# A two-block transformer in fp32 on one core: output turned tile by tile at the end, modulation in three pieces, strict order where the norm's steps run

## The chip, the cores and the metric

The kernel runs on one core of a Trainium2 chip. The metric is device time in microseconds, median of three runs. The engines are TensorE (PE, matmuls; PEld its weight loads), VectorE (DVE), ScalarE (ACT), GpSimd (POOL) and SyncE (SP), which issues the DMAs. A 128-partition memory (SBUF) feeds the engines, and matmuls write to PSUM.

## The reference

256 latent tokens (`x`) and 256 context tokens, width 1024, go through two blocks of two layers each. The first block's layers look like this (its second layer gives no context output):

```python
mod = silu_c @ w_mod[l] + b_mod[l]                     # 6 x 1024 per stream
sh1, sc1, g1, sh2, sc2, g2 = jnp.split(mod, 6)
a = modulate(rms_norm(h, norm1_g[l]), sh1, sc1)        # y * (1 + scale) + shift
p, u, vs, q, k, v, gl = jnp.split(a @ w_in[l], SPLIT_POINTS)
# three branches: pooling mix, spatial gating, neighbourhood attention over latent + context
h = h + g1 * merge_branches(...)
h = h + g2 * sq_relu_mlp(modulate(rms_norm(h, norm2_g[l]), sh2, sc2), w_ff1[l], w_ff2[l])
# at the block's end: rms_norm(h, final_g)
```

The second block has one layer with an mLSTM mixer (two directions, chunks of 128) and one with sliding-window attention (SWA, 16 heads, window 128, sinks), each with modulation and MLP (width 4096) in the same manner, and ends with `rms_norm(h, final_g)` of the 256 latent tokens, which is the output (256 x 1024).

## The kernel before

**Layout.** The residual lies transposed in SBUF as `h[128, 8, 512]`: eight row tiles `k` of 128 features, columns 0 to 255 the context, 256 to 511 the latent tokens. A matmul in fp32 is made of three: each operand is split into a high part (`whi`, by an ACT copy, L118) and a low part (`wlo`, by a subtraction, `split`, L132); high x high, high x low and low x high are added up in PSUM. A weight tile is 128 x 1024 (512 KB), loaded by SP (`staged`, L143), and its halves are made by ACT and, as `wlow` says, by DVE or POOL.

**Order.** The kernel is written in Python in the order wanted; a list scheduler puts each engine's instructions in order: among those that are ready in its own model of the machine, the earliest written goes first (`sooner` moves some up). An engine then works its queue strictly in that order. `issue_after(ins)` adds an edge to the scheduler's order alone: what is written under it is queued behind `ins`.

**Gemms.** `gemm` (L209) runs over weight tiles; `rows_of` (L164) writes, for each of the eight rows of an accumulation, the three matmuls (`mm`, L124). A group's first tiles may run side by side (`head`), the second two rows behind the first (SKEW). The last tiles of a gemm (`last_tiles`, L246) run the latent columns of all tiles first and then the context columns, so that the latent tokens' norm may start early. `Steps` (L47) is that norm as a Python generator, whose steps are taken at given ticks (rows) of other matmuls: `MID` (6, 12) in the second stream of the last tiles, `PRE` (4, 7) in the first matmuls of the next group ("head"), where the context's norm runs. Only where an instruction is given as `after` are the rows chained in written order.

**Norm.** `square` makes the squares by row tile (ACT, then sums on POOL, L551; the last two tiles by a pair addition on DVE, L558). `variance` (L564) makes the mean square per token in a column of PSUM, a power on POOL (L569), `rows` spreads it by four matmuls over partitions, and `modulate` makes the next group's inputs.

**Modulation.** For each of the four layers a vector of 1024 is multiplied with 1024 x 6144 weights, 352 units of 128 x 512 that are popped from a list (`pending`). A unit (L464) is a load of 256 KB, a product-addition on DVE into `a0` (context), a product on ACT and an addition on POOL into `a1` (latent, L480); after eight units 16 small matmuls and a reading out follow. `drip` (L502) pops units at a `rate` per weight tile; `need` pops what is missing before a value is used. There are three buffers for the loads and one pair of accumulators.

**Places.** `block1` (L873) is called twice (l = 0, 1); its context norm in layer 1 runs whole after the first three weight tiles. `block2_swa` (L1354) sets `wlow` to POOL for the weights of the query tiles. At the end of `build` the factor of the final norm is spread by `rows` over all partitions, eight DVE operations scale the row tiles and eight DMAs write the output transposed (`out_T`, L1471); the host turns it.

Of the kernel before, what the change touches and what calls it, by code (L numbers as in the profile page):

```python
# [19 lines left out]
P = 128  # L20
D = 1024
KT = 8
# [15 lines left out]
FIRST = (3, 3, 3, 3, 5, 7, 7, 7, 7), (2, 2, 2, 2, 4, 6, 6, 6, 6), (1, 1, 1, 1, 3)  # L38

WARM = 40  # L40
PRE, MID = (4, 7), (6, 12)
PLAIN = (3, 6)

SOONER = 70
# [2 lines left out]
class Steps:  # L47
# [5 lines left out]
    def tick(self):  # L53
# [3 lines left out]
            ins = next(self.parts, None)  # L57
        return ins

    def finish(self):  # L60
        for _ in self.parts:
            pass


class Builder:
    def __init__(self, tc, io, stack):
        self.tc, self.nc, self.io = tc, tc.nc, io
        self.n = 0
        self.pending, self.owed, self.rate = [], 0.0, 0.0
        self.raws = cycle(["raw"])  # L70
# [93 lines left out]
    def rows_of(self, pss, tiles, ks_of, xs, r0, r1, a, e, steps=None, after=None):  # L164

        last = len(xs) - 1
        order = after and (lambda ins=after: self.tc.issue_after(ins.ins))
        strict = bool(after)  # L170
        for i in range(r0, r1 + SKEW * (len(tiles) - 1)):
            for j, (ps, (d, w)) in enumerate(zip(pss, tiles)):
                i0 = i - SKEW * j
                if not r0 <= i0 < r1:
                    continue
                k = ks_of(d)[i0]
                wh, wl = (x[:, k * P:(k + 1) * P] for x in w)
                xh, xl = (x[:, a:e] for x in xs[i0])
                with order() if order else nullcontext():
                    self.mm(ps, wh, xh, start=(i0 == 0), stop=False)  # L180
                    self.mm(ps, wh, xl, start=False, stop=False)
                    ins = self.mm(ps, wl, xh, start=False, stop=(i0 == last))
            if strict:
                with self.tc.issue_after(ins.ins):
                    part = steps.tick()
                ins = part or ins
                order = lambda ins=ins: self.tc.issue_after(ins.ins)
            elif steps:
                steps.tick()
        return ins  # L190

    def group(self, tiles, ks_of, xs, cols, evac, steps=None):


        for a, e in cols:
            pss = [self.ps(next(self.banks))[:, :e - a] for _ in tiles]
            self.rows_of(pss, tiles, ks_of, xs, 0, len(xs), a, e, steps)
            self.flush()
            self.take(pss, tiles, a, e, evac)

    def take(self, pss, tiles, a, e, evac):

# [4 lines left out]
                    self.late.append(part)  # L207

    def gemm(self, aps, xs, c0, evac, head=0, tail=0, order=(LAT, CTX), pre=None, mid=None, flush=True,  # L209
             ahead=(), streams=True):  # L210

# [7 lines left out]
        while i < n - tail:  # L219
            m = max(head, 1) if i == 0 else 1  # L220
            cols = by_stream if streams and m > 1 and not self.ready else [(c0, T)]
            tiles = [(i + j, self.ready.pop(0) if self.ready else self.wload(aps[i + j], kt))
                     for j in range(m)]
            if i + m == n:
                self.ready = [self.wload(ap, KT) for ap in ahead]
            steps = Steps(pre, PRE) if pre and i == 0 else None
            self.group(tiles, ks_of, xs, cols[:1], evac, steps)
            if steps:
                steps.finish()
            self.group(tiles, ks_of, xs, cols[1:], evac)  # L230
            for _ in range(1 if m == 1 else 0 if streams else m):
                self.drip()
            i += m
# [11 lines left out]

    def last_tiles(self, tiles, ks_of, xs, by_stream, evac, mid):  # L246
        steps = Steps(mid, MID) if mid else None
        for s, cols in enumerate(by_stream):
            for tile in tiles:
                self.group([tile], ks_of, xs, [cols], evac, steps if s else None)  # L250
        if steps:
            steps.finish()

# [204 lines left out]
    def mod_units(self, i, groups):  # L458
# [3 lines left out]
        w, sc = self.io[f"wmod{i}"], self.silu[i // 2]  # L462

        def unit(cg, half, k):  # L464
            raw = self.staged(w[cg, k][:, half * 512:half * 512 + 512], 512, cycle(["mraw"]))
            a0, a1 = self.macc[:, 0], self.macc[:, 1]

            alone = i % 2 == 1 and cg >= 2
            if not alone or k % 2 == 0:
                s = LAT if alone else CTX  # L470
                if k == 0:
                    self.nc.vector.tensor_scalar_mul(a0, raw, sc[:, k, s:s + 1])
                else:
                    self.stt(a0, raw, sc[:, k, s:s + 1], a0, ALU.mult, ALU.add)
            if not alone or k % 2:
                if k < 2 - (not alone):
                    self.act(a1, raw, scale=sc[:, k, LAT:LAT + 1])
# [17 lines left out]
        out = []  # L495
        for cg in groups:
            for half in range(2):
                out += [((i, cg), (lambda cg=cg, half=half, k=k: unit(cg, half, k)))
                        for k in range(KT)]
        return out  # L500

    def drip(self):  # L502
# [5 lines left out]
        self.owed = min(self.owed, 1.0)  # L508

    def one(self):  # L510
        self.pending.pop(0)[1]()

    def need(self, i, cg):

        while any(key == (i, cg) for key, _ in self.pending):
            self.one()
        while self.late:
            self.flush()

# [181 lines left out]
        return evac  # L701


    def mlp(self, i, xs, c0, tag, pre=None, mid=None, other=None, gain=None, rows=None):


        w1, w2 = self.io[f"ff1_{i}"], self.io[f"ff2_{i}"]
# [37 lines left out]
            hid[q] = hs  # L745

        def down(q, **kw):
            self.gemm2([w2[q, d] for d in range(4)], hid.pop(q), c0, self.add_to_h(g2, q == 7, gain), **kw)

        self.raws = cycle(["raw", "Y", "Y"])  # L750
        up(0, head=3, pre=pre)
# [121 lines left out]
def block1(b, ph, l, xs, pre, after):  # L873
# [12 lines left out]
        b.perm1 = b.load(ph, "perm1")  # L886
        b.icnt = b.load(ph, "icnt")
    pscale = b.vec[l][:, 64:66]
    b.rate = 0.0 if l else RATES[l][0]
    win = io[f"win{l}"]  # L890

    qs, kh, kl = [], [], []
# [55 lines left out]
    if l == 0:  # L948
        pre(evac_first)
    else:  # L950
        b.gemm(aps[:3], xs, c0, evac_first, head=3)
        b.ready = [b.wload(ap, KT) for ap in aps[3:]]
        b.whole(pre)
        b.gemm(aps[3:4], xs, c0, lambda j, *r: evac_first(j + 3, *r))
    b.gemm_rows(aps[4:], L, xs, ("T", "T", "S", "S")[c0 // P:], evac_vs, c0=c0)
    br = b.new_xs("B", 4)
# [394 lines left out]
    b.mlp(i, xs, 0, "A", pre=b.norm(xs, CTX, A, S), **after)  # L1351


def block2_swa(b, ph, xs, pre):  # L1354
    nc, io = b.nc, b.io
    i = 3
    rope2 = b.load(ph, "rope2")
# [35 lines left out]
    def project(t):  # L1393
        b.gemm([win[t]], xs, L, lambda _, ps, a, e: qs.append(query(ps)))

    b.wlow = nc.gpsimd
    project(0)
    for t in range(8):
        if t < 7:
            project(t + 1)  # L1400
        a = b.new_xs("A", 1)[0]
# [19 lines left out]
    b.mlp(i, xs, L, "A", pre=b.factors(R), rows=R)  # L1421


def build(tc, io):
    from contextlib import ExitStack

    with ExitStack() as stack:
# [35 lines left out]
            st, pre, mid = follow(3, "B")  # L1463
            block2_mlstm(b, ph, xs2, b.norm_twice(xs2, A, S), dict(mid=mid))
        with tc.tile_pool(name="b3", bufs=1) as ph:
            block2_swa(b, ph, st["xs"], pre())
        R = b.rstd_rows(LAT)
        for k in range(KT):
            t = b.T1()
            b.stt(t, b.h[:, k, L:], b.fin[:, 8 + k:9 + k], R, ALU.mult, ALU.mult)  # L1470
            nc.sync.dma_start(io["out"][:, k, :], t)  # L1471

# [149 lines left out]
```

## Time and profile before

| | |
|---|---|
| runs | 2252.66, 2251.72, 2252.01 us; median 2252.01 |
| profiled execution | 2251.2 us, span 2249.3 us, 36790 instructions |
| mean granted clock of TensorE | 0.986 |
| PE busy | 2179.0 us, 97% |
| DVE busy | 1617.5 us, 72% |
| ACT busy | 1155.4 us, 51% |
| POOL busy | 642.3 us, 29% |

The span is the time from the profile's first to its last instruction on the core. Busy times are the sums of an engine's own instructions; PE's matmuls are pipelined, and their ends are modelled. The granted clock is the share of TensorE's full speed that it was given: 1.00 in most of the span, lower in a few stretches. In a timeline's row stand the start in us, the busy time in us, engine, line, operation, output<-inputs by the program's names, shape and count; a bracket gives the engine's idle time before it and what ended that.

### The profile page before, as it was taken

How to read it: one execution, taken by the hardware profiler on the slowest of the kernel's cores; microseconds unless marked ns; L12 is line 12 of the kernel's file. 1: busy time of each engine (PE TensorE's matmuls, PEld its weight loads, DVE VectorE, ACT ScalarE, POOL GpSimd, SP SyncE). 2: the span in 40 equal slices, each digit the busy share in tenths (PEclk: the TensorE clock that was granted, in tenths of full speed). 3: DMA queues.
4: the chain of work that ended last, by engine and by line, in shares of the span. 5: the costliest groups of instructions: out<-in, count | busy, mean ns of one | idle time of the engine just before them, and what ended most of it. 6: DMA issues, size and time to landing. Idle time of an engine off the chain costs nothing.

```text
span 2249.3 us, 36790 instructions
## 1 busy us (share of the span) xinstructions
PE 2179.0 (97%) x13602; PEld 1861.3 (83%) x13602; DVE 1617.5 (72%) x2830; ACT 1155.4 (51%) x2176; POOL 642.3 (29%) x529
## 2 busy tenths in 40 slices
PE   9899999999999989998999999999999999999998
PEld 7777877887777778898999977778777778879998
DVE  5876656777666986789777766678775566697776
ACT  4556434544443456655555665645444433676453
POOL 1630534524221542045000234262232122421000
PEclk9999999999999999999999999999999999999999
DMA  8451535445565443367554323444455552214552
GB/s 296 140 167 36 169 122 190 144 133 183 191 193 162 147 154 127 120 215 254 166 186 151 113 85 104 142 142 131 137 187 177 173 168 80 76 48 143 186 179 93
DMA packets 129011, 337.86 MB, mean 150 GB/s; under 512 B 15040, under 2 KB 24256, under 8 KB 128832
## 3 DMA queue, kind: packets, MB, share of 16 engines
q1 hardware_dynamic: 128832, 335.51, 46.0%
q8 instruction: 108, 1.77, 0.3%
q14 instruction: 71, 0.58, 0.1%
HBM read 334.40 MB, written 1.05 MB: 149 GB/s over the span
## 4 chain that ended last, share of the span: by engine, by line
PE 46%; DVE 4%; ACT 2%; issue 2%; POOL 1%; DMA 0%; DVEq 0%; POOLq 0%; ACTq 0%
PE mm L124 28%; PE mx L124 11%; PE S L124 2%; PE T L124 1%; PE num L124 1%; PE pv L124 1%; PE T L128 1%; DVE wlo L132 1%; ACT whi L118 1%; PE acc L124 0%; POOL macc L480 0%; DMA mraw<-wmod_in 0%; PE kv L124 0%; DVE B L121 0%; ACT W L118 0%
## 5 line engine op out<-in xcount | busy, mean ns | idle before, releaser
L124 PE MATMUL mm<-A,whi 128*128 128x512 f32 (+2 forms) x2632 | 666.2, 340 | 4.9 <-DVE A L121 1.5
L480 POOL TENSOR_TENSOR macc<-macc,mraw 128x512 f32<-128x512 f32 x244 | 361.9, 1483 | 757.3 <-ACT mraw L118 744.8
L124 PEld LDWEIGHTS mm<-A,whi 128*128 128x128 f32 x2632 | 449.3, 190 | 69.0 <-issue 10.0
L124 PE MATMUL mm<-B,whi 128*128 128x512 f32 (+2 forms) x1916 | 461.4, 331 | 2.8 <-DVE h L121 1.0
L132 DVE TENSOR_TENSOR wlo<-raw,whi 128x1024 fp32r<-128x1024 f32 x255 | 350.8, 1378 | 140.7 <-ACT whi L118 139.6
L124 PE MATMUL mm<-A,wlo 128*128 128x512 f32 (+2 forms) x1316 | 444.4, 338 | 1.2 <-DVE wlo L132 1.2
L118 ACT ACTIVATE whi<-raw 128x1024 fp32r<-128x1024 f32 x267 | 281.2, 1055 | 250.5 <-PE mm L124 154.6
L124 PEld LDWEIGHTS mm<-B,whi 128*128 128x128 f32 x1916 | 322.1, 189 | 41.8 <-issue 3.0
L118 ACT ACTIVATE mraw<-mraw,silu 128x512 f32<-128x512 f32 x244 | 175.5, 723 | 303.1 <-DVE macc L121 181.3
L124 PE MATMUL mx<-A,whi 128*128 128x512 f32 (+2 forms) x1272 | 323.3, 341 | 5.5 <-ACT whi L118 4.2
L124 PE MATMUL mm<-B,wlo 128*128 128x512 f32 (+2 forms) x958 | 315.2, 330 | 1.1 <-DVE wlo L132 1.1
L121 DVE SCALAR_TENSOR_TENSOR macc<-mraw,silu,macc 128x512 f32<-128x512 f32 x244 | 250.2, 1025 | 58.8 <-DMA mraw<-wmod_in 56.3
L124 PEld LDWEIGHTS mm<-A,wlo 128*128 128x128 f32 x1316 | 249.4, 190 | 29.2 <-DVE wlo L132 2.0
L132 DVE TENSOR_TENSOR wlo<-Y,whi 128x1024 fp32r<-128x1024 f32 x160 | 207.7, 1298 | 78.7 <-ACT whi L118 78.5
L118 ACT ACTIVATE whi<-Y 128x1024 fp32r<-128x1024 f32 x160 | 168.9, 1055 | 177.8 <-PE mm L124 124.7
L124 PEld LDWEIGHTS mx<-A,whi 128*128 128x128 f32 x1272 | 218.6, 190 | 35.1 <-ACT whi L118 4.4
L124 PE MATMUL mx<-A,wlo 128*128 128x512 f32 (+2 forms) x636 | 216.3, 340 | 0.7 <-DVE wlo L132 0.7
L124 PE MATMUL mx<-B,whi 128*128 128x256 f32 (+2 forms) x852 | 203.9, 327 | 3.0 <-DVE B L121 1.3
L124 PEld LDWEIGHTS mm<-B,wlo 128*128 128x128 f32 x958 | 181.1, 189 | 19.9 <-DVE wlo L132 2.0
L121 DVE SCALAR_TENSOR_TENSOR h<-mm,mod,h 128x256 f32<-128x256 f32 x278 | 125.5, 478 | 65.0 <-PE mm L124 64.6
L124 PEld LDWEIGHTS mx<-B,whi 128*128 128x128 f32 x852 | 144.3, 191 | 19.9 <-DVE B L121 2.7
L551 POOL TENSOR_TENSOR sums<-sums,T 128x256 f32<-128x256 f32 x60 | 65.6, 1100 | 307.5 <-ACT T L118 306.3
(331 smaller groups left out, 3009.8 us busy)
## 6 DMA issues: line engine op xcount, KB each, us to landing
mraw<-wmod_in SPq DMA_DIRECT2D x352, 256.0 KB, 2.9
Y<-ff_in SPq DMA_DIRECT2D x160, 512.0 KB, 3.6
raw<-ff_in SPq DMA_DIRECT2D x96, 512.0 KB, 3.5
raw<-win_in SPq DMA_DIRECT2D x68, 512.0 KB, 3.8
raw<-mwin_in SPq DMA_DIRECT2D x17, 512.0 KB, 3.5
raw<-wo_in SPq DMA_DIRECT2D x16, 512.0 KB, 4.3
raw<-swin_in SPq DMA_DIRECT2D x10, 512.0 KB, 3.5
B<-wfirst_in SPq DMA_DIRECT2D x16, 256.0 KB, 6.7
```

The source lines that it names most:

```text
L118: return self.nc.scalar.activation(out, in_, func, **kw)
L121: return self.nc.vector.scalar_tensor_tensor(out, a, scalar, b, op0, op1)
L124: return self.nc.tensor.matmul(out, lhsT=lhsT, rhs=rhs, start=start, stop=stop, **kw)
L128: return self.nc.tensor.transpose(out, in_, self.ident[:k, :k])
L132: (eng or self.nc.vector).tensor_sub(lo, src, hi.bitcast(F32))
L480: self.nc.gpsimd.tensor_add(a1, a1, raw)
L551: (adder or self.nc.gpsimd).tensor_add(sums, sums, sq)
```

## The change

Six things are done:

1. In the last MLP each finished row tile of the residual is scaled by the final norm's gain (ACT) and transposed by two matmuls into four PSUM banks, written behind the next tile's matmuls. At the end the variance is kept per partition (token), four 128 x 512 copies out of PSUM scale by it (two on DVE, two on ACT), and four DMAs of 256 KB write the output, which has its final layout.
2. A modulation unit is a generator of three pieces: the load, the DVE product, the rest (ACT, POOL). Popping a unit writes the rest of the unit before, the loads of this one and the next one, and this one's DVE product.
3. Wherever steps run, the rows are chained as written and the steps are queued behind their tick; in the last tiles' second stream the chain goes from tile to tile until the steps are done, and MID is (8, 14).
4. In layer 1 of the first block the context's norm runs as steps at ticks 2 and 5 of the first three tiles' matmuls, and the next weights are loaded ahead.
5. The modulation's rate is 0 at the beginning of both of the first block's layers, before only of the second.
6. In SWA, `wlow` is POOL from the query tile t = 2 on; the low halves of the first two query tiles' weights are made on DVE.

```diff
-PRE, MID = (4, 7), (6, 12)
+PRE, MID = (4, 7), (8, 14)
+NEXT = (2, 5)
...
+    def done(self):
+        return self.n >= self.at[-1]
...
-        strict = bool(after)
+        strict = bool(after or steps)
...
                 order = lambda ins=ins: self.tc.issue_after(ins.ins)
-            elif steps:
-                steps.tick()
         return ins
...
-            self.rows_of(pss, tiles, ks_of, xs, 0, len(xs), a, e, steps)
+            ins = self.rows_of(pss, tiles, ks_of, xs, 0, len(xs), a, e, steps, after)
...
-            steps = Steps(pre, PRE) if pre and i == 0 else None
+            steps = Steps(pre, at) if pre and i == 0 else None
...
+        last = None
         for s, cols in enumerate(by_stream):
             for tile in tiles:
-                self.group([tile], ks_of, xs, [cols], evac, steps if s else None)
+                due = s and steps and not steps.done()
+                ins = self.group([tile], ks_of, xs, [cols], evac, steps if due else None,
+                                 last if due else None)
+                last = ins
...
         def unit(cg, half, k):
             raw = self.staged(w[cg, k][:, half * 512:half * 512 + 512], 512, cycle(["mraw"]))
+            yield
             a0, a1 = self.macc[:, 0], self.macc[:, 1]
...
                     self.stt(a0, raw, sc[:, k, s:s + 1], a0, ALU.mult, ALU.add)
+            yield
             if not alone or k % 2:
...
     def one(self):
-        self.pending.pop(0)[1]()
+        self.rest()
+        self.begun = self.pending.pop(0)[1]
+        for piece in [self.begun] + [u for _, u in self.pending[:1]]:
+            if piece not in self.loaded:
+                next(piece)
+                self.loaded.append(piece)
+        self.loaded.remove(self.begun)
+        next(self.begun)
+
+    def rest(self):
+        if self.begun:
+            next(self.begun, None)
+        self.begun = None
 
     def need(self, i, cg):
         while any(key == (i, cg) for key, _ in self.pending):
             self.one()
+        self.rest()
...
-    b.rate = 0.0 if l else RATES[l][0]
+    b.rate = 0.0
...
-        b.gemm(aps[:3], xs, c0, evac_first, head=3)
-        b.ready = [b.wload(ap, KT) for ap in aps[3:]]
-        b.whole(pre)
+        b.gemm(aps[:3], xs, c0, evac_first, head=3, pre=pre, at=NEXT, ahead=aps[3:])
...
-    b.wlow = nc.gpsimd
     project(0)
     for t in range(8):
+        if t == 1:
+            b.wlow = nc.gpsimd
...
-        R = b.rstd_rows(LAT)
-        for k in range(KT):
-            t = b.T1()
-            b.stt(t, b.h[:, k, L:], b.fin[:, 8 + k:9 + k], R, ALU.mult, ALU.mult)
-            nc.sync.dma_start(io["out"][:, k, :], t)
+            outs = []
+            def turned(k):
+                if not outs:
+                    outs.extend(b.ps(tag) for tag in ("S", "S", "acc", "T"))
+                t = b.T1()
+                b.act(t, b.h[:, k, L:], scale=b.fin[:, 8 + k:9 + k])
+                def rest():
+                    cols = slice(k % 4 * P, (k % 4 + 1) * P)
+                    for j in range(2):
+                        b.tr(outs[2 * (k // 4) + j][:, cols], t[:, j * P:(j + 1) * P])
+                b.late.append(rest)
+            block2_swa(b, ph, st["xs"], pre(), turned)
+            b.flush()
+            r = b.variance(LAT)
+            for half in range(2):
+                for j in range(2):
+                    o, ps, f = b.t("W" if half else "E"), outs[2 * half + j], r[:, j:j + 1]
+                    if j:
+                        b.act(o, ps, scale=f)
+                    else:
+                        nc.vector.tensor_scalar_mul(o, ps, f)
+                    nc.sync.dma_start(
+                        io["out"][j * P:(j + 1) * P, half * T:(half + 1) * T], o)
```

## Rows read from the trace of the kernel before

**Rows 1.** The page, parts 1 and 5: busy times; POOL's modulation additions.

```profile
PE 2179.0 (97%) x13602; PEld 1861.3 (83%) x13602; DVE 1617.5 (72%) x2830; ACT 1155.4 (51%) x2176; POOL 642.3 (29%) x529
...
L480 POOL TENSOR_TENSOR macc<-macc,mraw 128x512 f32<-128x512 f32 x244 | 361.9, 1483 | 757.3 <-ACT mraw L118 744.8
```

**Rows 2.** Windows: length, PE, PEld, DVE, ACT, POOL busy, clock, DMA share, GB/s.

```profile
50.00:100.00 50.00, 44.27 (x263) 37.29 (x262) 41.83 (x54) 25.03 (x42) 30.79 (x23) 0.93 0.43 136
800.00:850.00 50.00, 41.89 (x293) 37.83 (x292) 43.82 (x73) 27.40 (x48) 20.68 (x21) 0.90 0.45 151
1500.00:1550.00 50.00, 44.71 (x329) 42.16 (x328) 39.67 (x69) 25.73 (x52) 18.91 (x15) 0.93 0.35 109
1700.00:1750.00 50.00, 50.00 (x229) 39.72 (x228) 29.41 (x44) 20.80 (x30) 11.17 (x8) 1.00 0.56 177
1900.00:1950.00 50.00, 43.96 (x288) 41.30 (x287) 28.26 (x58) 25.53 (x57) 19.17 (x14) 0.86 0.26 85
```

**Rows 3.** Timeline of the end, from the last matmul on.

```profile
2237.97 0.28 PE L124 MATMUL mx<-A,wlo 128*128 128x256 f32 x1
...
2240.84 0.71 POOL L569 TENSOR_TENSOR sm<-sm,m 128x2 f32<-128x2 f32 x1 [3.58 <-DVE sm L568]
...
2242.35 3.22 DVE L121 SCALAR_TENSOR_TENSOR T<-h,fin,T 128x256 f32<-128x256 f32 x8 [1.59 <-PE T L124]
2242.86 3.79 SPq L1471 DMA_DIRECT2D out_T<-T  x8
```

**Rows 4.** Instructions of line 128 (transposes): ns min/median/max, first and last start.

```profile
L128 PE MATMUL T<-ident,T x48: 270/270/421, 21.4 to 1878.3; 128*128 128x128 f32 x48
```

**Rows 5.** Timeline in SWA: four transposes in a row.

```profile
1960.62 0.60 PE L128 MATMUL T<-ident,E 128*128 128x128 f32 x4
```

**Rows 6.** Timeline at layer 0's beginning.

```profile
81.29 0.72 ACT L118 ACTIVATE mraw<-mraw,silu 128x512 f32<-128x512 f32 x1 [4.28 <-DVE sm L942]
82.86 0.57 ACT L118 ACTIVATE E<-mm 128x512 f32<-128x512 f32 x1
83.49 1.22 PE L124 MATMUL T<-E,perm 128*128 128x256 f32 x2 [5.73 <-ACT E L118]
...
90.13 0.68 DVE L966 TENSOR_TENSOR B<-S,sgb 128x512 f32<-128x512 f32 x1
```

**Rows 7.** DMA issues: count, KB each, median us to landing.

```profile
mraw<-wmod_in SPq DMA_DIRECT2D x352, 256.0 KB, 2.9
...
B<-wfirst_in SPq DMA_DIRECT2D x16, 256.0 KB, 6.7
...
out_T<-T SPq DMA_DIRECT2D x8, 128.0 KB, 2.0
```

**Rows 8.** Timeline of PE at layer 1's start.

```profile
831.16 1.22 PE L124 MATMUL mx<-A,whi 128*128 128x512 f32 x2 [4.19 <-ACT whi L118]
...
835.24 0.58 PE L124 MATMUL S<-wlo,A 128*128 128x256 f32 x1 [2.85 <-DVE wlo L132]
```

**Rows 9.** Timeline in the mLSTM layer's tail.

```profile
1508.82 0.75 DVE L121 SCALAR_TENSOR_TENSOR macc<-mraw,silu,macc 128x512 f32<-128x512 f32 x1 [3.19 <-DMA mraw<-wmod_in]
...
1512.12 0.53 PE L124 MATMUL T<-mean,T 128*128 128x1 f32 x2 [3.69 <-DVE T L558]
```

**Rows 10.** Timeline at SWA's first query tiles.

```profile
1919.76 2.37 POOL L132 TENSOR_TENSOR wlo<-raw,whi 128x1024 fp32r<-128x1024 f32 x1 [4.22 <-ACT whi L118]
...
1923.76 0.39 PE L124 MATMUL mm<-whi,B 128*128 128x256 f32 x1 [2.06 <-ACT T L118]
...
1940.98 0.49 PE L124 MATMUL S<-Q,Q 128*128 128x512 f32 x1 [1.64 <-DVE Q L121]
```

**Rows 11.** Timeline of DVE in the first MLP's head.

```profile
437.70 1.21 DVE L132 TENSOR_TENSOR wlo<-Y,whi 128x1024 fp32r<-128x1024 f32 x1
```

**Rows 12.** The chain of waits: start, us, a run of 48 matmuls of 128x256.

```profile
1929.70 5.70 PE mm L124 x48
```

**Rows 13.** Window of the first MLP's head, columns as in rows 2.

```profile
434.00:447.00 13.00, 12.15 (x105) 11.07 (x103) 11.83 (x24) 8.28 (x19) 3.76 (x3) 1.00 0.37 121
```

More of the change, by code (lines that the diff above doesn't have):

```diff
@@ L69, in __init__ @@
         self.pending, self.owed, self.rate = [], 0.0, 0.0
+        self.begun, self.loaded = None, []
         self.raws = cycle(["raw"])
@@ L187, in rows_of, with group @@
                 order = lambda ins=ins: self.tc.issue_after(ins.ins)
-            elif steps:
-                steps.tick()
-        return ins
-    def group(self, tiles, ks_of, xs, cols, evac, steps=None):
+        return ins
+    def group(self, tiles, ks_of, xs, cols, evac, steps=None, after=None):
+        ins = None
         for a, e in cols:
             pss = [self.ps(next(self.banks))[:, :e - a] for _ in tiles]
-            self.rows_of(pss, tiles, ks_of, xs, 0, len(xs), a, e, steps)
+            ins = self.rows_of(pss, tiles, ks_of, xs, 0, len(xs), a, e, steps, after)
             self.flush()
             self.take(pss, tiles, a, e, evac)
+        return ins
     def take(self, pss, tiles, a, e, evac):
@@ L209, in gemm @@
     def gemm(self, aps, xs, c0, evac, head=0, tail=0, order=(LAT, CTX), pre=None, mid=None, flush=True,
-             ahead=(), streams=True):
+             ahead=(), streams=True, at=PRE):
         kt, n = len(xs), len(aps)
@@ L497, in mod_units @@
             for half in range(2):
-                out += [((i, cg), (lambda cg=cg, half=half, k=k: unit(cg, half, k)))
-                        for k in range(KT)]
+                out += [((i, cg), unit(cg, half, k)) for k in range(KT)]
         return out
@@ L701, in add_to_h, with mlp @@
         return evac
-    def mlp(self, i, xs, c0, tag, pre=None, mid=None, other=None, gain=None, rows=None):
+    def mlp(self, i, xs, c0, tag, pre=None, mid=None, other=None, gain=None, rows=None, then=None):
         w1, w2 = self.io[f"ff1_{i}"], self.io[f"ff2_{i}"]
@@ L747, in down @@
         def down(q, **kw):
-            self.gemm2([w2[q, d] for d in range(4)], hid.pop(q), c0, self.add_to_h(g2, q == 7, gain), **kw)
+            self.gemm2([w2[q, d] for d in range(4)], hid.pop(q), c0, self.add_to_h(g2, q == 7, gain, then if q == 7 else None), **kw)
         self.raws = cycle(["raw", "Y", "Y"])
@@ L1351, in block2_mlstm, with block2_swa @@
     b.mlp(i, xs, 0, "A", pre=b.norm(xs, CTX, A, S), **after)
-def block2_swa(b, ph, xs, pre):
+def block2_swa(b, ph, xs, pre, then):
     nc, io = b.nc, b.io
@@ L1420, in block2_swa @@
     R = []
-    b.mlp(i, xs, L, "A", pre=b.factors(R), rows=R)
+    b.mlp(i, xs, L, "A", pre=b.factors(R), rows=R, then=then)
 def build(tc, io):
@@ L1465, in build @@
         with tc.tile_pool(name="b3", bufs=1) as ph:
-            block2_swa(b, ph, st["xs"], pre())
-        R = b.rstd_rows(LAT)
-        for k in range(KT):
-            t = b.T1()
-            b.stt(t, b.h[:, k, L:], b.fin[:, 8 + k:9 + k], R, ALU.mult, ALU.mult)
-            nc.sync.dma_start(io["out"][:, k, :], t)
+            outs = []
[21 more added lines that the diff above has]
+                        io["out"][j * P:(j + 1) * P, half * T:(half + 1) * T], o)
 def _tiles(w):
@@ L1617 @@
                             kind="ExternalInput").ap() for n, v in arrays.items()}
-    io["out"] = nc.dram_tensor("out_T", (P, KT, L), F32, kind="ExternalOutput").ap()
+    io["out"] = nc.dram_tensor("out_T", (L, D), F32, kind="ExternalOutput").ap()
     with tile.TileContext(nc) as tc:
@@ L1622 @@
     out = np.asarray(r.results[0]["out_T"])
-    return np.ascontiguousarray(out.transpose(2, 1, 0).reshape(1, L, D))
+    return np.ascontiguousarray(out.reshape(1, L, D))
```

## The prediction

> **What bounds the kernel now.** The page's busy times come first: TensorE (PE) is busy 97% of the span, the vector engine 72%, and the modulation's POOL additions (244 of 1483 ns) are a long side stream [rows 1]. A change that leaves the matrix work as it is can only gain in the remaining 3%, or in the clock. So the stretches of 50 us come second: in 1700 to 1750 PE is busy for all 50 us at a clock of 1.00, while around the block boundaries it is busy for 41.9 to 44.7 us of 50 and the granted clock averages 0.86 to 0.93 [rows 2]. At such places PE waits some microseconds, and then works for a while at the lower of its two levels, 1.2 instead of 2.4 GHz. What the low level costs I read as (1 - granted) times the window: 3.5 us in 50 to 100, 5.0 in 800 to 850, 3.5 in 1500 to 1550, 7.0 in 1900 to 1950. Third, the timelines of these places give the waits themselves; each part below has its own. Last, after the final matmul a tail of 11 us runs with PE nearly empty [rows 3].
>
> The sums go against the profiled execution: 2251.2 us, of which 2249.3 span and 1.9 around it. The median of the runs shown is 2252.0, 0.8 above; I add that at the end.
>
> **The end.** Before: the last matmul ends at 2238.25, its residual tile, square and variance follow; the power on POOL ends at 2241.55; four matmuls spread the factor over the partitions, eight DVE products of 0.40 us make the tiles, eight DMAs go out, the last issued at 2246.65; the span ends at 2249.3, so 2.65 us after that issue [rows 3]. The change removes the spreading and the eight products. In their place stand two rounds of scaled 128x512 copies out of PSUM, one on DVE beside one on ACT. Such a copy took 0.57 us on ACT and such an operation 0.68 on DVE [rows 6], so 2241.55 + 2 x 0.7 = 2243.0 and the last issue at about 2243.1, 3.5 earlier. The DMAs are 256 KB instead of 128 KB: before, 2.0 us to landing for the 128 KB; 256 KB took 2.9 as a median of the modulation's loads and 6.7 in the crowd at the start [rows 7]. That is 0.9 to 4.7 more. Added on the path: 16 transposes, 14 of them among the last matmuls, the last two after the last residual tile, beside the squares. One lone transpose lasts 0.27 us [rows 4], but four in a row 0.60 [rows 5], a step of (0.60 - 0.27)/3 = 0.11 us; 14 x 0.11 = 1.5. The eight ACT copies that feed them lie beside the matmuls of the following tile. Gain 3.5 - 0.9 - 1.5 = 1.1; with the slow landing -2.7, with transposes wholly under the wait for the weights +2.6. I take **+1**, nearest to the loads with the same long rows.
>
> [...]
>
> **Rate 0 at layer 0's beginning.** Nine of the modulation's units (a load, a DVE product, an ACT product, a POOL addition) no longer run before the v projection's matmuls; all later ones are up to ten units later. At 83.5 PE waits 5.73 us for ACT's E, which stood on ACT behind a unit's product that itself had waited 4.28 us for DVE [rows 6]. The low clock then costs 3.5 us [rows 2]. Ends: nothing, if E's other producers are as late, and 5.7 + 3.5 = 9.2. The units are only one of the two things on that chain, so I take **+4**.
>
> **Layer 1's start.** The context's norm no longer runs whole between the third and the fourth weight tile, but in the first three tiles' matmuls. PE's waits there are 4.19 us and 2.85 us [rows 8], and the low clock costs 5.0. The ends are +12 and, if the same DVE work merely delays the three tiles' own weight halves, +1. I take **+7**: the vector engine is busy 43.8 of 50 us [rows 2], so the work is not free, but the matmuls of three tiles cover it.
>
> **mLSTM's tail.** Of the units, what ran into this tail is now either done earlier (the output projection's gate must be complete before it, which forces a burst of some eight units there) or later. The wait is 3.69 us at 1512.1, behind a DVE pair addition that came after a unit's DVE product, which had waited 3.19 us for its load [rows 9]. With the load issued one unit ahead and the product apart from the rest, that wait should go: +3.7, and some of the 3.5 us of clock. Against it stands the burst of eight POOL additions of 1.48 = 12 us beside the matmuls of the gates. From 0 to +7; **+4**.
>
> **SWA's first two query tiles.** Their weights' low halves move from POOL to DVE. A POOL half took 2.37 us [rows 10], one on DVE 1.21 [rows 11]. PE's waits there are 2.06 and 1.64 us [rows 10], and the low level costs another 3 to 4 of the stretch's 7. DVE gets two more instructions of 1.21 in a stretch in which it is busy 28 of 50 us. 0 to +7; **+4**.
>
> **Strict order in tails and heads.** In the tails the norm's steps come 2 ticks later; a tick is three 128x256 matmuls at 0.119 us [rows 12], so 0.7 us later. In the next group's head PE may no longer take rows in any order: the matmuls are queued behind the steps in their order. Four heads of this kind (at about 434, 815, 1523, 1902). In the first the rows of the new tiles start about where the window of [rows 13] does, and PE then runs the first tile's rows ahead, since the next tile's low half is made only at 437.70 + 1.21 = 438.9 [rows 11]; in the 13 us from 434 PE is busy 12.15, idle 0.85 [rows 13]. As written, three rows of the first tile are nine matmuls, 1.07 us, until 435.1; then it waits up to 3.8 us for the second tile. Only if DVE makes the half earlier is the wait shorter, and DVE is busy 11.83 of those 13 us [rows 13]. What speaks for less: the steps' own matmuls no longer go ahead of rows that could run, and the modulated tiles come in the order in which the rows want them. Per head 0 to -4; I take -2, between, and four times that: **-8**.
>
> **The rest**, the units in three pieces elsewhere: their products stand on DVE, ACT and POOL all the same, PE is saturated beside them (clock 1.00, [rows 2]): **0**, within 3 either way.
>
> Sum: 1 + 4 + 7 + 4 + 4 - 8 = 12. 2251.2 - 12 = 2239.2, plus 0.8: **2240 us**. Taken alone this case has 2229 to 2250, some two thirds of each term up or down.
>
> **Rivals.**
> A, slower: the strict heads starve PE. Each waits 3.8 us, and PE then falls to 1.2 GHz for a stretch that costs 3.5 (as in 50 to 100 and 1500 to 1550, after waits of 5.7 and 3.7). Four times 7.3 is 29; the gains of 20 leave -9: 2261. It decides by when the second tile's low half is there: from some 3 us after the first tile's nine matmuls on. For it: DVE's fullness in these heads. Against: the low half can be put ahead of the modulated tiles on DVE, as it has slack afterwards.
> B, no change: the waits only move. E, the gate's load and the first query halves have a second producer nearly as late; early rate and mLSTM give 0, SWA 2, layer 1 4, the end 1, against -6: +1, 2251. For it: at 83.5 ACT's product before E was itself waiting for DVE [rows 6], and this DVE work partly stays.
> C: every wait and its half clock goes (2.6 + 9 + 12 + 7 + 7, of which I leave four fifths, 30) and the heads cost nothing: 2222. For it: the waits' listed releasers are just what the change moves. Against: so far as DVE is the bottleneck in 800 to 850, moving its work does not shrink it.
>
> **How the numbers follow.** Forecast 0.50, A 0.19, B 0.18, C 0.13. The range reaches from C's place to just beyond A's: 2222 to 2262. This kernel's measurement tells 0.2%, 4.5 us, from no change: same is 2247.5 to 2256.5. Of the forecast's 0.50 some 0.06 lies there; of B nearly all, 0.02 of it on either side taken together; of A 0.01. Faster 0.44 + 0.13 + 0.01 = 0.58, same 0.06 + 0.16 + 0.01 = 0.23, slower 0.19.
>
> **What would show it.** The 50 us windows at 50, 800, 1500 and 1900 should have a higher granted clock than 0.93, 0.90, 0.93, 0.86 and PE busier; 83.5's wait under 3 us; the waits of 4.19 and 2.85 at layer 1's start gone or under 2 together; 1512's under 1; the tail from last matmul to end under 11 us, transposes included. Wrong it is if PE's idle before the second tile's first row in the heads at 434, 815, 1523 and 1902 adds up to over 10 us, or if the clock falls in the head at 434, where it was 1.00 [rows 13].

## The result, and the profile after

The changed kernel takes 2268.8 us (median of four runs, 2264.5 to 2271.0) beside 2251.9 for the kernel before: a ratio of 1.0076, interval 1.0061 to 1.0091. It is slower by 17 us where 12 less were forecast. The profiled execution has a span of 2267.2, 17.9 more than before, and takes 2268.97.

The page's busy times of the changed kernel: PE is busy 8.5 us longer than in [rows 1], and in a span longer by 17.9 it is idle 9.4 us more. The granted clock of the whole span is 0.983 instead of 0.986; (1 - granted) times the span, that is some 7 us more. So about half of the loss is new waiting, and most of the other half is work done at the lower clock.

```profile
PE 2187.5 (96%) x13614; PEld 1870.0 (82%) x13614; DVE 1610.8 (71%) x2826; ACT 1162.1 (51%) x2186; POOL 623.7 (28%) x527
```

Its windows (columns as in [rows 2]) show where:

```profile
50.00:100.00 50.00, 43.51 (x248) 37.10 (x247) 43.55 (x53) 24.98 (x42) 30.76 (x23) 0.93 0.41 130
400.00:450.00 50.00, 43.84 (x303) 40.13 (x302) 34.38 (x55) 24.24 (x45) 28.43 (x23) 0.90 0.47 151
800.00:850.00 50.00, 42.55 (x311) 40.91 (x310) 40.43 (x70) 26.52 (x52) 22.64 (x22) 0.86 0.49 156
1500.00:1550.00 50.00, 45.33 (x314) 41.73 (x314) 35.30 (x59) 24.28 (x47) 27.60 (x22) 0.93 0.44 140
1900.00:1950.00 50.00, 45.31 (x336) 43.58 (x336) 29.78 (x64) 25.11 (x57) 9.77 (x11) 0.90 0.17 57
```

Against [rows 2] the places that were to get better stay where they were: the clock is 0.93 again at 50, 0.86 instead of 0.90 at 800, 0.93 again at 1500, and a little better only at 1900. And a new one has come: the stretch 400 to 450, which in the kernel before has PE busy 48.59 us at a clock of 1.00:

```profile
400.00:450.00 50.00, 48.59 (x360) 44.03 (x359) 41.05 (x68) 26.65 (x52) 27.12 (x21) 1.00 0.45 143
```

Where the time is lost is best seen as a lag: at equal sums of matmul columns done by PE, how much later than the kernel before a kernel is (worked out from all PE records of the two traces; single traces differ by up to some 4 us without cause, see the last section).

```
us before    changed   units alone   rate alone   strict alone   without strict
   402        -0.8        +2.0          -1.6          -2.1            -1.2
   463        +6.8        +6.6          +2.4          -0.1            +2.5
   793        +8.0        +5.8          +3.4          -0.7            +3.2
   892       +13.5        +5.7          +4.6          +1.1            +4.5
  1021       +12.2        +8.2          +5.1          +1.3            +3.7
  1086       +17.3       +11.2         +15.9          +1.9            +9.5
  1288       +17.1       +11.2         +16.3          +2.4            +9.1
  1324       +13.0       +16.4         +12.2          -0.5            +5.1
  1607       +15.7       +16.3         +13.7          +0.2            +6.0
  2211       +18.2       +16.3         +15.6          +2.4            +4.7
```

The first loss is 7.6 us between 402 and 463. Its timeline in the changed kernel, DVE and then PE:

```profile
421.35 1.48 DVE L127 SCALAR_TENSOR_TENSOR macc<-mraw,silu,macc 128x512 f32<-128x512 f32 x1 [1.45 <-DMA mraw<-wmod_in]
422.99 0.75 DVE L127 SCALAR_TENSOR_TENSOR macc<-mraw,silu,macc 128x512 f32<-128x512 f32 x1 [0.17 <-DMA mraw<-wmod_in]
424.95 0.75 DVE L127 SCALAR_TENSOR_TENSOR macc<-mraw,silu,macc 128x512 f32<-128x512 f32 x1 [1.22 <-DMA mraw<-wmod_in]
425.62 0.48 DVE L127 SCALAR_TENSOR_TENSOR h<-mm,g,h 128x256 f32<-128x256 f32 x1
426.92 1.53 DVE L585 TENSOR_TENSOR T<-T,T 128x256 f32<-128x256 f32 x1 [0.82 <-POOL macc L493]
...
428.51 0.59 PE L130 MATMUL T<-mean,T 128*128 128x1 f32 x2 [3.33 <-DVE T L585]
...
442.64 0.39 PE L130 MATMUL mx<-A,wlo 128*128 128x256 f32 x1 [2.72 <-DVE wlo L138]
...
821.71 0.38 PE L130 MATMUL T<-mean,sums 128*128 128x1 f32 x2 [2.40 <-POOL sums L578]
...
1539.05 0.39 PE L130 MATMUL mm<-B,wlo 128*128 128x256 f32 x1 [2.91 <-DVE wlo L138]
...
1920.11 0.58 PE L130 MATMUL mm<-B,wlo 128*128 128x256 f32 x1 [2.29 <-DVE wlo L138]
```

Two things are to be seen. At 421 to 425 the modulation's products stand on DVE ahead of the residual tile `h` and wait for their loads; so the last residual tile, the pair addition behind it and PE's variance come late, 3.33 us. It is just the wait of [rows 9], in another layer. The other four are the four heads: PE waits 2.7, 2.4, 2.9 and 2.3 us, 10.3 together, in three of them for the second tile's low half, as rival A has it, and at 821.71 for POOL's sums.

### The profile page after: what moved, and what is told of

Read it like the earlier page. It is cut to its first block, busy times and chain, and to the rows that moved or that the text cites. A ratio compares the mean times of both kernels' runs of the same rounds, so it can differ in the third digit from the quotient of the medians.

```text
span 2267.2 us, 36808 instructions
## 1 busy us (share of the span) xinstructions
PE 2187.5 (96%) x13614; PEld 1870.0 (82%) x13614; DVE 1610.8 (71%) x2826; ACT 1162.1 (51%) x2186; POOL 623.7 (28%) x527
## 5 line engine op out<-in xcount | busy, mean ns | idle before, releaser
L493 POOL TENSOR_TENSOR macc<-macc,mraw 128x512 f32<-128x512 f32 x244 | 353.8, 1450 | 663.4 <-ACT mraw L124 652.5
```

Of the source, the lines that this page charges most:

```text
L493: self.nc.gpsimd.tensor_add(a1, a1, raw)
```

## The experiments

Each ratio is to runs of the kernel before on the same chip. "Alone" is the kernel before with one part of the change.

| run | what | ratio, interval |
|---|---|---|
| end_alone | the end | 1.0008 (0.9998, 1.0017) |
| units_alone | units in three pieces | 1.0090 (1.0075, 1.0105) |
| strict_alone | strict order, MID | 1.0037 (1.0015, 1.0059) |
| without_strict | change less strict order and MID | 1.0038 (1.0024, 1.0052) |
| units_ahead | only the load a pop ahead | 0.9986 (0.9975, 0.9998) |
| units_late | only the rest a pop late | 1.0081 (1.0063, 1.0099) |
| next_alone | layer 1's start | 0.9997 (0.9984, 1.0010) |
| without_units | change less units | 1.0098 (1.0083, 1.0113) |
| rate_alone | rate 0 | 1.0077 (1.0057, 1.0096) |
| without_rate | change less rate 0 | 1.0113 (1.0092, 1.0135) |
| without_units_rate | change less both | 1.0024 (1.0012, 1.0036) |
| ahead_end_next | ahead, end, layer 1's start | 1.0000 (0.9986, 1.0013) |
| rate_made_up | rate 0, then 1.65 for 1.4 | 1.0033 (1.0020, 1.0045) |
| rate_lower | 1.2 for 1.4 in layer 0's attention | 1.0050 (1.0030, 1.0070) |
| strict_pool | strict order, low halves on POOL | 1.0059 (1.0037, 1.0081) |
| swa_alone | SWA's low halves | 0.9989 (0.9979, 0.9999) |
| ahead_swa | ahead, SWA | 0.9988 (0.9974, 1.0001) |
| ahead_swa_end | ahead, SWA, end | 0.9978 (0.9966, 0.9989) |

**First: which part?** After the traces I held that the strict order costs the time (theory S), with the units' pieces as the rival (theory U). Four kernels: the end alone, the units alone, the strict order alone (the hunks of the change's diff for that part), and the changed kernel with `strict = bool(after)`, the tails unchained and MID (6, 12).

> Only the end of the kernel as changed (row tiles turned one by one, factor per partition), all else as before. In the changed kernel the tail from the last residual matmul on is 2.7 us shorter than its lag before it would make it. Both theories: 2 to 3 us faster than before, 2249 to 2250, and no other place of the trace moves.

> Only the modulation's units in three pieces, all else as before. Theory S (the strict order costs the time): within 3 us of before, 2249 to 2255. Theory U (the units' pieces, which now stand in front of other work on DVE, ACT and POOL, cost the time): 6 to 14 us slower, 2258 to 2266, with waits of PE of 2 to 3 us in the middle of layers, as at 425, 874 and 1055 of the changed kernel.

> Only the rows in written order wherever the norm's steps run, the tails' second stream chained, MID (8, 14); all else as before. Theory S: four heads in which PE waits 2.3 to 2.9 us for the second tile's low half (10 us in all) and the clock's fall in those where it was 1.00 (5 us), less what the tails lose as waits: 8 to 15 us slower, 2260 to 2267. Theory U: the order as such costs little, since the scheduler had much the same one: within 4 us of before.

> The changed kernel with the rows' order and MID as before, all other parts kept. Theory S: the 17 us go and some of the forecast's gains show, 2242 to 2252. Theory U: still 2262 to 2268.

Measured: 1.0008, 1.0090, 1.0037 and 1.0038. S falls as the main cause: the strict order alone costs 7.3 us, just under what S said, and without it the rest still loses 7.6. But U isn't right either: both of these runs (2255.6 and 2255.9 us) lie between the ranges of the two theories, and the units alone lose 21 (2269.0 us), more than U said and more than the whole change. The 2.7 us that the first expectation reads off were an error of mine: the lag counts columns, and the end's own columns differ. By the spans of the two traces the end wins 0.3 us (lag 18.2 before it, 17.9 in the span).

In the units' run the largest single wait is 5.88 us. PE, DVE, ACT, POOL, SP of that stretch:

```profile
1329.85 1.13 PE L127 MATMUL kv<-Q,T 128*64 128x129 f32 x8 [5.88 <-ACT Q L121]
...
1323.42 0.75 DVE L124 SCALAR_TENSOR_TENSOR macc<-mraw,silu,macc 128x512 f32<-128x512 f32 x1 [7.35 <-DMA mraw<-wmod_in]
1324.09 1.22 DVE L135 TENSOR_TENSOR wlo<-raw,whi 128x1024 fp32r<-128x1024 f32 x1
...
1324.25 0.72 ACT L121 ACTIVATE mraw<-mraw,silu 128x512 f32<-128x512 f32 x1 [4.88 <-DVE macc L124]
1324.88 0.58 ACT L121 ACTIVATE Q<-S 128x512 f32<-128x512 f32 x1
...
1312.12 6.73 POOL L1256 TENSOR_TENSOR T<-Q,cols 128x128 f32<-128x128 f32 x12
...
1319.50 4.02 POOL L486 TENSOR_TENSOR macc<-macc,mraw 128x512 f32<-128x512 f32 x3
...
1320.83 3.05 SPq L146 DMA_DIRECT2D mraw<-wmod_in  x3
```

Read from below: the load is issued at 1320.83, when the first POOL addition has given a buffer back; the additions stood behind 6.73 us of other POOL work; the product on DVE waits 7.35 us for that load, ahead of a weight's low half; ACT's product waits for DVE's, ahead of `Q`, which PE needs.

**Second: load ahead, or rest late?**

```diff
-        for piece in [self.begun] + [u for _, u in self.pending[:1]]:
+        for piece in [self.begun]:                    # units_late
...
         next(self.begun)
+        self.rest()                                   # units_ahead
```

> As the units alone, but a unit's ACT and POOL part is written in the same pop as its DVE product, as before; only the load of the next unit is written one pop ahead. In the run with the units alone PE waited 5.9 us at 1324, since a unit's DVE product stood ahead of a weight's low half and waited 7.35 us for its load, whose buffer waited for POOL. Theory L (the load written ahead lets the scheduler put the product too early on DVE): still 10 to 20 us slower than before. Theory P (the part that is written a pop late holds the three buffers longer): within 4 us of before.

> As the units alone, but each unit's load is written at its own pop; only the ACT and POOL part comes a pop late. Theory L: within 4 us of before. Theory P: 10 to 20 us slower. If both halves cost a part each, some 5 to 10.

1.0081 for the late rest, 0.9986 for the load ahead: what costs is the late rest, as theory P has it. The load ahead is a gain of 3 us, the rest written a pop later a loss of 18. That it costs by holding the buffers is shown at one place: in the kernel with the late rest alone the wait of 1324 is there again, and so is the product's wait for its load.

```profile
1327.58 1.13 PE L127 MATMUL kv<-Q,T 128*64 128x129 f32 x8 [5.92 <-ACT Q L121]
...
1321.15 0.75 DVE L124 SCALAR_TENSOR_TENSOR macc<-mraw,silu,macc 128x512 f32<-128x512 f32 x1 [7.39 <-DMA mraw<-wmod_in]
```

Reckoned as in the table, this kernel's trace is 15.1 us behind at 2211. Of these 5.7 arise between 1288 and 1324, and 5.2 between 402 and 463, in the tail of which the next part tells.

With these ran the start of layer 1 (`pre=pre, at=NEXT, ahead=aps[3:]`) alone, and the change with whole units:

> Only layer 1's start as changed: the context's norm as steps at ticks 2 and 5 of the first three tiles, the next weights loaded ahead; the rows in the scheduler's order as before. My forecast's term was 7 us faster. If it holds, 2239 to 2245 beside a before of 2248; the rival is that the same DVE work only delays the weights' halves, within 3 us of before, with waits at 826 to 835 of the same sum of 7 us.

> The changed kernel with the modulation's units whole as before; all else as changed. If the units cost the time as they do alone (20 us), within 4 us of before, 2245 to 2253. If the strict order costs as much beside the other parts, 2255 to 2262.

Layer 1's start is 0.9997: neither a gain nor a loss. The change without its units is 1.0098 (2272.4 us, above both of its ranges), no better than with them. So the cost isn't the units' alone, and the parts don't add.

**Third: the rate.**

> Only the rate 0 at the beginning of layer 0. The forecast gave it a gain of 4 us. Rival, from the units counted in the trace (before: 68 of 244 DVE products by 410 us, changed: 56): all units come ten later, a whole group of eight falls into the tail before 425, where DVE waits for the group's loads ahead of the variance's pair addition and PE waits 3.3 us: 5 to 12 us slower, most of it between 400 and 465 and near 875; and the wait at 83 stays, since other units move up into it.

> The changed kernel with the rate of before at layer 0's beginning. If the rate is what costs beside the strict order: 8 to 15 us faster than the changed kernel, 2253 to 2260. If the late part of the units costs by itself, the wait at 428 stays and it is 2264 to 2270.

> The changed kernel with whole units and the rate of before: end, strict order, layer 1's start, SWA's weights. If units and rate are the whole cost, 2240 to 2250. If the strict order costs by itself, as in the run with it alone (7 us), 2252 to 2260.

> A version from the parts that did not lose: the end as changed, layer 1's start as changed, loads of the units one pop ahead with the rest at once. If the parts add up (0, 0 and 3 us), 2243 to 2248; if the order that the scheduler then finds is another one, within 6 us of before either way.

`b.rate = 0.0` alone is 1.0077, a loss of 18 us where I had forecast a gain of 4, and more than the rival's 5 to 12; taking it out of the change makes that slower still (1.0113: 2275.7 us, beyond both of the expected ranges), and taking both units and rate out leaves 1.0024 (2254.9 us, in the second range). The version of the parts that did not lose is at 1.0000: the 3 us of the load ahead don't show beside the other two. Rate alone +18, late rest alone +18, both together, with the other parts but not the strict order, +7.6. One thing is common: the wait in the tail at 425. The rate's run, DVE and PE:

```profile
424.04 0.96 DVE L123 SCALAR_TENSOR_TENSOR macc<-mraw,silu,macc 128x512 f32<-128x512 f32 x1 [1.21 <-DMA mraw<-wmod_in]
424.92 0.47 DVE L123 SCALAR_TENSOR_TENSOR h<-mm,g,h 128x256 f32<-128x256 f32 x1
426.20 0.43 DVE L560 TENSOR_TENSOR T<-T,T 128x256 f32<-128x256 f32 x1 [0.82 <-POOL macc L482]
...
426.69 0.38 PE L126 MATMUL T<-mean,T 128*128 128x1 f32 x2 [2.94 <-DVE T L560]
```

The windows of the accumulators' instructions alone (410 to 432, the tail before the first MLP) show what falls there: PE's 16 matmuls are a group's reading out, DVE's count its products. In order: before, load ahead, rate made up; then changed, rest late, rate 0, rate lower (the made-up and the lower rate are described further below).

```profile
410.00:432.00 22.00, 0.00 (x0) 0.00 (x0) 5.35 (x5) 0.00 (x0) 8.68 (x6) 1.00 0.45 138
```
```profile
410.00:432.00 22.00, 0.00 (x0) 0.00 (x0) 5.48 (x5) 0.00 (x0) 9.96 (x7) 1.00 0.41 138
```
```profile
410.00:432.00 22.00, 0.00 (x0) 0.00 (x0) 8.08 (x7) 0.30 (x1) 9.88 (x7) 1.00 0.53 171
```
```profile
410.00:432.00 22.00, 0.64 (x16) 0.38 (x16) 7.62 (x8) 0.72 (x1) 8.62 (x6) 0.89 0.40 134
```
```profile
410.00:432.00 22.00, 0.64 (x16) 0.38 (x16) 9.18 (x8) 0.71 (x1) 10.32 (x7) 0.97 0.42 144
```
```profile
410.00:432.00 22.00, 0.64 (x16) 0.38 (x16) 7.88 (x8) 0.71 (x1) 9.65 (x7) 0.92 0.38 131
```
```profile
410.00:432.00 22.00, 0.65 (x16) 0.38 (x16) 8.98 (x8) 0.71 (x1) 8.72 (x6) 1.00 0.46 145
```

There is one pair of accumulators, so no unit of a group starts until the one before is read out. With twelve units fewer by then (56 products by 410 instead of 68), or with the last POOL addition a pop late (64), the border of two groups lies in the tail; the next group's units follow close behind it (in the rate's run eight products within 15 us), with three buffers between them.

Over the traces of all 20 kernels the wait goes with the border. In the eight that read a group out between 410 and 414 us, PE waits 2.2 to 3.8 us for the pair addition; in the twelve that read it out at 408 or before, it doesn't wait for it at all.

But this tail isn't where the rate alone loses most. In the table it loses 4.0 us between 402 and 463, and 10.7 of its 15.6 between 1021 and 1086, on the way into layer 1's MLP. The same windows from 1040 to 1090, in order: before, rate made up, rest late, rate 0.

```profile
1040.00:1090.00 50.00, 0.00 (x0) 0.00 (x0) 4.36 (x5) 0.00 (x0) 10.52 (x7) 0.97 0.60 193
```
```profile
1040.00:1090.00 50.00, 0.00 (x0) 0.00 (x0) 5.56 (x6) 0.44 (x1) 11.60 (x7) 0.97 0.62 197
```
```profile
1040.00:1090.00 50.00, 0.64 (x16) 0.38 (x16) 6.65 (x8) 0.72 (x1) 10.40 (x7) 1.00 0.64 213
```
```profile
1040.00:1090.00 50.00, 0.64 (x16) 0.38 (x16) 8.10 (x8) 0.71 (x1) 10.27 (x7) 0.83 0.56 184
```

Here too a border has moved: the rate's run reads a group out at 1054 us, the kernel before at 1033, and the clock is 0.83 instead of 0.97. But the late rest has a border in this window as well, at 1043, keeps a clock of 1.00 and loses only 1.9 us between 1021 and 1086. So a border near by isn't enough, and what makes this stretch slow with rate 0 isn't shown.

**Fourth: the count, and the heads.**

```diff
-RATES = ((1.4, 2.0), ...
+RATES = ((1.65, 2.0), ...     # rate_made_up, with b.rate = 0.0 at the beginning
+RATES = ((1.2, 2.0), ...      # rate_lower, beginning as before
...
-                     for j in range(m)]
+             # strict_pool: self.wload(aps[i + j], kt, self.nc.gpsimd if j else None)
```

> Rate 0 at layer 0's beginning, and 1.65 instead of 1.4 after it, so that the count of units by the tail at 425 us is that of before. Theory G (what costs is where the groups fall): back to within 5 us of before, with no wait of 2.9 us at 424. Theory B (rate 0 at the beginning costs by itself, whatever comes after): still 12 to 20 us slower.

> The beginning of layer 0 as before, but 1.2 instead of 1.4 units per weight tile in all its attention part: fewer units by the tail at 425, as with rate 0 at the beginning. Theory G: 8 to 20 us slower, with a wait of 2 to 4 us at 424. Theory B: within 4 us of before.

The lower rate: 1.0050, with the border in the tail (56 products by 410) and a wait of 3.79 us before the variance. Made up: 1.0033, no border in the tail (65 products by 410) and no wait there. Between 402 and 463 and between 1021 and 1086 the lower rate loses 6.0 and 8.9 us, the made-up one 1.2 and nothing. And the late rest (64 products by 410, wait of 2.96 us) and the made-up rate (65, no wait) differ by one product: in the tail it is the border that counts, not the number. So where the groups fall matters, with rate 0 and without it; of the 18 us of rate 0, eleven came back with the count. The other seven did not: theory G said 5 at most, and what is left lies elsewhere (the lag rises to 4.9 already by 402). Whether rate 0 at the beginning or the denser units after it are to blame for these seven is open.

> The strict order alone, but in each head the second and third weight tile's low half is made on POOL, beside DVE. If PE's waits of 2.7 to 3.4 us in the heads at 434, 824, 1523 and 1898 are DVE's low half behind the modulated tiles, they go, and the run is 5 to 10 us faster than the strict order alone (2255): 2245 to 2250. If POOL's 2.4 us half or the high half is as late, the waits stay at 2 us or more and the time within 3 us of 2255.

1.0059 (2263.6 us, above both ranges), no faster than the strict order alone (1.0037; the intervals overlap). The wait for the low half is gone, and in its place stands one for the modulated tile itself, in the first head:

```profile
438.20 0.39 PE L129 MATMUL mm<-A,whi 128*128 128x256 f32 x1 [1.86 <-DVE A L126]
```

With the strict order alone it was 2.79 there, for the low half. That fits DVE's work in a head being needed in full by then, whichever of its products comes last; it isn't tested further, and the rest of the loss I did not follow up.

> Only the first two query tiles' low halves on DVE. My forecast's term was 4 us faster: 2243 to 2247 beside 2249, the waits of 2.06 and 1.64 us at 1924 and 1941 gone. The rival: another producer is as late there, within 2 us of before, as the changed kernel's 1.01 and 2.14 us there suggest.

0.9989: a gain of 3.0 us by the medians, 2.5 by the ratio, with an interval from 0.2 to 4.7. It is the only gain of mine that a run alone bears out, in its lower half.

**Last: what is left over as a gain.**

> The kernel before with the units' loads one pop ahead (ACT and POOL part at once) and SWA's first two low halves on DVE. Alone they gave 2.8 and about 2.7 us. If they add up, 5 us faster than before: about 2245 beside 2250. If what one finds is lost by the other's order, within 2 us of before. No wait of PE over 1 us in the tail at 425 in either case.

> The same with the end as changed. From the last residual matmul on its lag falls by 2.7 us, so if it adds up 2242 to 2244. Alone the end gave no gain in the median (+1.8, from 10 runs that spread over 8 us): then within 1 us of the run beside it.

0.9988 (its interval still takes in no change) and 0.9978 (2246.6 beside 2250.6): with the end the version is 4 us faster than the kernel before. Whether the end is worth anything in it can't be told: the intervals overlap.

## Why the prediction was wrong, step by step

Two steps failed: the gain of 4 for rate 0, and the nothing for the units in three pieces. Each costs 18 us alone.

**Rate 0 at layer 0's beginning, "+4".** Alone it costs 17.7 us. The wait at 83 that it was to remove stayed, and grew, in the changed kernel as in the run with rate 0 alone (6.49 us in both):

```profile
84.15 1.22 PE L130 MATMUL T<-E,perm 128*128 128x256 f32 x2 [6.49 <-ACT E L124]
```

The accumulators' instructions from 50 to 84 us, before and changed:

```profile
50.00:84.00 34.00, 0.00 (x0) 0.00 (x0) 9.65 (x8) 0.58 (x1) 10.47 (x7) 0.97 0.41 132
```
```profile
50.00:84.00 34.00, 0.00 (x0) 0.00 (x0) 11.01 (x8) 0.71 (x1) 8.95 (x6) 0.98 0.40 128
```

DVE makes eight products ahead of the wait in both: other units have come up into the place of those that were to go. And what the edit did do, all later units "up to ten" later (twelve by 410), I wrote down as a count and then gave no price. "Later" is not free for work in groups of eight with one accumulator: it moves the borders of the groups, and one came to lie in a tail in which the residual's chain leaves no slack. That tail is 4 of the 15.6 us of the trace; of the 10.7 between 1021 and 1086 it is shown that they go when the count is made up, but not by which wait they come.

**The rest, the units in three pieces, "0, within 3 either way".** Their late rest alone costs 18 us, in part by the same mechanism (5.2 us around the tail at 425) and in part by the held buffer of 1324 (5.7): "their products stand on DVE, ACT and POOL all the same" is true of the sums and wrong of the order. PE's saturation in 1700 to 1750 was read from a stretch that is not where the groups' borders hurt.

**Strict heads, "-8".** Right in kind, and in size as far as it was measured: -7.3 alone, with an interval from 3 to 13, and waits of 2.3 to 2.9 us in the changed kernel. The profiled run of the strict order alone was only 2.7 us slower than that of the kernel before, so its trace doesn't show where all of the seven lie. Rival A, which had the sign, is not what happened. Both of the signs of being wrong came: 10.3 us of waits in the heads, and in the first one a clock of 0.89 from 434 to 447 instead of 1.00 [rows 13]. But the strict order gives 7 us and not 29.

**Layer 1's start, "+7".** Alone 0, with waits of 1.40 and 5.26 us in place of the 4.19 and 2.85 of [rows 8]: the sum is 6.7 instead of 7.0. In the changed kernel the waits of [rows 8] became 2.67 us for a high half, and the wait at 821 came before it; the clock went from 0.90 to 0.86. This is the lower end that I had given (+1), the same DVE work merely delaying the weights.

```profile
840.74 0.79 PE L130 MATMUL S<-whi,A 128*128 128x256 f32 x2 [2.67 <-ACT whi L124]
```

**mLSTM's tail, "+4".** In the changed kernel the variance no longer waits its 3.69 us [rows 9]; PE waits 1.12 us shortly before, and the head behind took 2.91 (above): moved, as rival B has it. The lag over this part is unchanged to within 2 us. Nor is it the load ahead that removed the wait, as I had it: with the load ahead alone it is still there (the second row), with the late rest (3.53) and with both (3.51) too, and it is gone with rate 0 or the lower rate, and back where the count is made up (3.19).

```profile
1520.29 0.48 PE L130 MATMUL mm<-A,whi 128*128 128x256 f32 x2 [1.12 <-ACT T L124]
```
```profile
1509.69 0.59 PE L127 MATMUL T<-mean,T 128*128 128x1 f32 x2 [3.51 <-DVE T L579]
```

**SWA, "+4".** Alone the edit gives some 3 us, and the clock from 1900 to 1950 is 0.97 there instead of 0.86. In both runs the first wait of [rows 10], 2.06 us, is gone; PE's next one is 1.0 us, in the changed kernel for ACT's `Q`. The second, 1.64 us, is ended by DVE's `Q` as before and has grown to 2.14 in the changed kernel, and DVE is the engine that got more work.

```profile
1949.87 0.51 PE L130 MATMUL mm<-B,whi 128*128 128x256 f32 x2 [1.01 <-ACT Q L124]
...
1959.03 0.49 PE L130 MATMUL S<-Q,Q 128*128 128x512 f32 x1 [2.14 <-DVE Q L127]
```

**The end, "+1".** About 0.3 by the spans, nothing measurable alone. The rows of the end, last residual matmul to last issue, and the DMAs' landing:

```profile
2257.76 0.29 PE L130 MATMUL mx<-A,wlo 128*128 128x256 f32 x1
...
2259.54 0.33 PE L134 MATMUL acc<-ident,T 128*128 128x128 f32 x1 [1.15 <-ACT T L124]
...
2261.56 0.75 DVE L1518 TENSOR_SCALAR E<-S,sm 128x512 f32<-128x512 f32 x1 [0.82 <-POOL sm L596]
...
2262.23 0.74 DVE L1518 TENSOR_SCALAR W<-acc,sm 128x512 f32<-128x512 f32 x1
...
2263.15 0.93 SPq L1519 DMA_DIRECT2D out_T<-W  x2
```
```profile
out_T<-E SPq DMA_DIRECT2D x2, 256.0 KB, 2.2
out_T<-W SPq DMA_DIRECT2D x2, 256.0 KB, 2.6
```

From the last residual matmul's end (2258.05) to the span's end are 9.15 us instead of 11.05 [rows 3]. The two rounds came as forecast, the landing a little sooner than the 2.9 assumed; but the 16 transposes, ACT's second copy of each tile and the last issue at 2264.1 leave a net of 0.3. A tail 1.9 us shorter and a net of 0.3 leave about 1.6 for the 14 transposes among the matmuls ahead of it, 0.11 each, as [rows 5] had it; this is an estimate from two single traces. The 275 ns of the Trainium skill (*TensorE: Matmul & The Clock Gate*, "Part 4: PE-mode transpose") is the length of one in the trace of the kernel before too (0.27, [rows 4]), not what one adds in a row (0.11, [rows 5]).

The sum itself was the last error. The terms were added as if each place were its own, and the 2229 to 2250 around their sum follows from no reckoning of theirs. Measured alone, the parts that lose come to 7, 18 and 21 us, and the change to 17; take one out and it gets better (the strict order) or no better (the units, the rate). The traces show why at two places. The tail at 425 is lost once, whether the rate, the late rest or both put the border there. And the wait of some 5.9 us near 1324 stands in the three kernels that have the late rest at the old rate, and not in the two that have it with rate 0. One list orders all engines, so an edit in one place can move the groups in every later layer.

## What to carry to other kernels

Before you price an edit that delays background work at nothing, ask where the borders of its batches will then lie: a batch that waits for one accumulator and starts all at once did no harm in the middle of a matmul stretch here, and cost 4 to 6 us around one tail. In an engine's queue a product that waits for its load blocks all that stands behind it; look for it ahead of the last link of each critical chain. And where one scheduler orders everything, run the parts one by one before adding them up.

## What the runs showed beyond that

The splitting of one unit's chain over two pops is the cost, not the earlier load: the same buffers with the load a pop ahead gain 3 us. And single runs of the kernel before spread far more than the three shown at first (2251.7 to 2252.7): the fastest and slowest of 23 were 2243.7 and 2255.2. The 0.2% that I took for what can be told holds for medians of many runs, not for one profile. Traces of two kernels whose waits agree can differ by 2 us in their first 170 us, as one wait of 2.1 us at 150 is there or not. And with the end alone, whose edit lies in the last MLP and behind it, the lag rises from -2.2 to +2.2 us between 1021 and 1086 and falls back to -0.5 by 1324.
